# Queries and keys transposed in 32x32 blocks by VectorE and exchanged through device memory; exponentials as a task step of their own

## The chip, the cores and the metric

One core of one Trainium2 chip runs the whole program in one launch. The metric is the device time of that launch in microseconds (us); the kernel before has a median of 3285.07 us over three runs (3284.50 to 3285.92). Engines are named as in the profile: PE (TensorE, matrix multiply), PEld (its weight load), DVE (VectorE), ACT (ScalarE), POOL (GpSimd) and SP (SyncE, which only issues DMAs here).

## The reference, cut to what matters

The input is a sequence of 256 tokens of width 2048, float32 throughout. Two blocks follow one another.

```
def first_block(x, ...):
    h = rms_norm(x) ; proj = h @ w_in           # 2048 -> 17488 columns
    # MLA attention, 16 heads: q, k = 128 "nope" + 64 rotary dims, RMS-normed per head, v = 128
    # FoX attention, 16 heads of 128: q, k RMS-normed, bias F_t - F_s from a cumulative forget gate
    y = concat(causal_attention(mla), causal_attention(fox))
    x = x + (y * sigmoid(gates)) @ w_out
    # PEER: 8 heads of product-key top-16 over 16384 one-neuron experts, dense here:
    x = x + (scattered_gates * gelu(h2 @ u.T)) @ v
def hybrid_layer(x, ...):                       # twice
    aq, ak, av, ag, bq, bk, bv, bg, cu, cglu, cg = split(x @ w_in)
    ya = diff_attention(aq, ak, av)   # 4 heads, two softmaxes of 64 dims each, a = p0 - lam * p1
    yb = dilated_attention(bq, bk, bv)  # 8 heads of 128, three dilated windows merged
    yc = conformer_conv(cu, cglu)     # GLU, causal depthwise conv of 31 taps, LayerNorm, swish, pointwise
    y = concat(ya*silu(ag), yb*silu(bg), yc*silu(cg)) @ w_out
    return layer_norm(ALPHA * x + y)
```

## The kernel before

**Jobs.** All large products run as one list of jobs. A job is one tile of weights of 512 x 512 (1 MB, 128 partitions x 2048), or a smaller one. It is cut into four pieces of 128 x 512. `load` brings the tile into a `raw` buffer (four of them, `AHEAD = 4`) by a DMA on SP's queue; `convert` splits each piece into a high part (`hi`, ACT, L208) and the rest (`lo`, DVE, L209), so that three fast matmuls per piece and token half (L260, L261, L263) give float32 accuracy. Eight `hi` and eight `lo` buffers let the conversion run seven pieces ahead of the matmuls (`PIECES = 7`). A piece is six matmuls of 512 columns. The load of job i+4 is issued when the conversion of job i is done.

**Tasks.** Everything else (norms, transposes, attention heads, the convolution) is written as Python generators, the tasks. `Tasks.step` is called once after each piece; such a step is called a tick here. In each of four lanes it continues the first task in the queue that is due, one step per lane and tick. `yield n` makes the task due n ticks later (`yield` alone: `apart`, by default 4), and no more than four tasks of a lane may be started and unfinished at a time. `flush` runs ticks at once, without matmuls between, until the named tasks are done; it stands where a job's `post` or `need` must have a result. The order of the instructions on each engine is the order in which this plan emits them.

**Queries and keys.** After the product of a query or key block (4 heads, 256 tokens) the raw result lies with tokens on partitions, and attention wants it with head dims on partitions. `to_heads` (L505) does this: `transposed` (L223) issues eight 128x128 transposes on PE (L230) in two PSUM tiles of the pool `side`, and ACT copies each half out with the norm's gain (L510, L512, or L185 with the two half masks for the differential keys `ak`). It is called for the 8 FoX blocks (`fox_norm`), the 8 MLA blocks (`mla_group`, where `rope_T` adds four transposes for the rotary part in the same step), the 12 blocks of the two hybrid layers (`heads_post`), and the 4 blocks of PEER queries.

**Attention heads.** `softmax_block` (L527) adds the bias and takes the row maxima on DVE (L533, L535), then the exponentials with their row sums on ACT (L537), all in one step; the reciprocal of the sums on DVE follows in the same step (L564, L1155, L1194). `weights_transposed` (three PE transposes, L544) and `values` come in later steps.

**The expert blocks already use an exchange.** `expert_in_jobs` transposes the activations in 32x32 blocks on DVE (L952), writes them to device memory by a DMA of POOL's queue (L954), and `weights_load` reads them back block by block by four DMAs (L963), so that tokens and experts have changed places.

Of the kernel before, what the change touches and what calls it, by code (L numbers as in the profile page):

```python
# [17 lines left out]
F32 = mybir.dt.float32  # L18
# [92 lines left out]
def hybrid_block_kernel(ctx: ExitStack, tc: tile.TileContext, a: dict, out: bass.AP):  # L111
# [5 lines left out]
    wp = ctx.enter_context(tc.tile_pool(name="wp", bufs=4))  # L117
    s4p = ctx.enter_context(tc.tile_pool(name="s4p", bufs=16))
# [39 lines left out]
    cst = kept([256], name="cst")  # L158
    A.dma_start(out=cst, in_=a["cst"][:, 0:256])
# [11 lines left out]
    ident, maskf = cst[:, 0:128], cst[:, 128:256]  # L171
# [4 lines left out]
    for c0 in (0, 256):  # L176
        V.tensor_copy(out=causal[:, c0:c0 + 128], in_=maskf)
# [125 lines left out]
    S = {}  # L303
# [166 lines left out]
    def forget_bias(g):  # L470
# [4 lines left out]
        mask = maskf[:, None, :].to_broadcast([P, 4, P])  # L475
# [29 lines left out]
    def to_heads(raw, gain):  # L505

        dst = s4([4, T])
        for pv, c in transposed(lambda c, tb: raw[:, tb, c * P:(c + 1) * P], 4):
            if gain is None:
                A.copy(out=dst[:, c:c + 2, :], in_=pv)  # L510
            else:
                A.activation(out=dst[:, c:c + 2, :], in_=pv, func=AF.Copy, scale=gain)  # L512
        return dst

    def fox_norm(key, raw, gain, post):
        def work():
# [6 lines left out]
            S[key] = to_heads(raw, gain)  # L523
            yield END
        return work()

    def softmax_block(sc, b0, b1, sums):  # L527

        pr = s2([384])
        mx, nmax = small(2), small(2)  # L530
# [8 lines left out]
        return pr  # L539
# [18 lines left out]
    def attention(parts, b0, b1, v, y, h):  # L558
# [3 lines left out]
        sums, rs = small(2), small(2)  # L562
        pr = softmax_block(sc, b0, b1, sums)
        V.reciprocal(out=rs, in_=sums)  # L564
        yield
        pts = weights_transposed(pr)
        yield
        o = values(pts, v, h)
        for tb in range(TB):
            V.tensor_scalar(out=y[:, tb, h * P:(h + 1) * P], in0=o[:, tb * P:(tb + 1) * P], scalar1=rs[:, tb:tb + 1],  # L570
                            scalar2=None, op0=OP.mult)
# [59 lines left out]
    def mla_group(g):  # L631
# [13 lines left out]
        def post_q(ps):  # L645
# [3 lines left out]
            def work():  # L649
# [13 lines left out]
                S["mq", g] = (to_heads(raw, vcol("mq")), rope_T(qr, False))  # L663
# [3 lines left out]
        def post_k(ps):  # L667
# [3 lines left out]
            def work():  # L671
# [13 lines left out]
                S["mk", g] = (to_heads(raw, vcol("mk")), rope_T(kr, True))  # L685
# [20 lines left out]
    def merged_task(key, m, scale):  # L706
# [4 lines left out]
        def work():  # L711
            for pv, c in transposed(lambda c, tb: m[:, tb, c * P:(c + 1) * P], 4):
                split_scaled(h[:, c:c + 2, :], l[:, c:c + 2, :], pv, scale)
# [3 lines left out]
    def gate_jobs(kind, g):  # L717
# [9 lines left out]
        def post(ps):  # L727
# [7 lines left out]
            merged_task(("m" + kind, g), z, 0.5)  # L735
# [91 lines left out]
    def peer_q_jobs():  # L827
# [5 lines left out]
        for b in range(4):  # L833
            def post(ps, b=b):
# [3 lines left out]
                def work():  # L838
                    qT = to_heads(raw, None)
# [271 lines left out]
    def layer(ly):  # L1111
# [3 lines left out]
        def heads_post(name, gain):  # L1115
            def post(ps):
                raw = raw_of(ps)

                def work():
                    if name != "ak":  # L1120
                        L[name] = to_heads(raw, gain)
                    else:
                        L[name] = [s4([4, T]), s4([4, T])]
                        for pv, c in transposed(lambda c, tb: raw[:, tb, c * P:(c + 1) * P], 4):
                            for i in range(2):
                                copy_scaled(L[name][i][:, c:c + 2, :], pv, halves[:, i:i + 1])
# [14 lines left out]
        def diff_post(ps):  # L1141
# [5 lines left out]
            def head(h):  # L1147
                q, k = L["aq"], L["ak"]
                prs, rs = [], []
                for c in range(2):  # L1150
                    sc = side()
                    qk(sc, [(q[:, h], k[c][:, h])])
                    sums, r = small(2), small(2)
                    prs.append(softmax_block(sc, *head_bias(h), sums))
                    V.reciprocal(out=r, in_=sums)  # L1155
                    rs.append(r)
                    yield 3
# [23 lines left out]
        def dil_post(b):  # L1181
            def post(ps):
# [5 lines left out]
                def head(h):  # L1188
# [3 lines left out]
                    sums, r = small(2), small(2)  # L1192
                    pr = softmax_block(sc, *head_bias(4 + 4 * b + h), sums)
                    V.reciprocal(out=r, in_=sums)  # L1194
                    yield 7
                    pts = weights_transposed(pr)
                    yield 7
# [409 lines left out]
```

## Time and profile before

| what | value |
|---|---|
| median of three runs | 3285.07 us (3284.50 to 3285.92) |
| the profiled execution, its own time | 3284.75 us |
| its span, first to last instruction | 3283.0 us |
| PE busy | 3258.2 us (99%) |
| PEld busy | 2706.0 us (82%) |
| DVE busy | 2359.3 us (72%) |
| ACT busy | 1743.4 us (53%) |
| POOL busy | 632.1 us (19%) |
| DMA moved | 676.54 MB, 206 GB/s; POOL's queue 60.45 MB |
| granted PE clock, mean | 0.998 of full speed |

The busy time of PE is a union of pipelined matmuls, whose ends are modelled: what an instruction costs PE is read from the starts of the matmuls around it, not from its duration. The span is 1.75 us shorter than the execution's own time. The first block with its attention takes until about 830 us, PEER until about 2310 us, the two hybrid layers the rest.

### The profile page before, as it was taken

What the parts mean: (1) busy time and instruction counts of PE and PEld (TensorE: products, weight loads), DVE (VectorE), ACT (ScalarE), POOL (GpSimd) and SP (SyncE); (2) the same over time, 40 slices, a digit from 0 to 9 for tenths busy, and PEclk for the clock granted to TensorE, in tenths of its full rate; (3) what the DMA queues carried; (4) which work ended last, traced back from release to release, by engine and by line L of the source; (5) the groups of instructions that cost most, each with busy time, mean ns of one, the idle gap of its engine ahead of it and who ended that gap; (6) DMA issues with size and microseconds to landing.
All of it is one profiled execution on the core that took longest, in us unless ns stands there. A gap on an engine that the chain in (4) does not pass through costs nothing.

```text
span 3283.0 us, 42983 instructions
## 1 busy us (share of the span) xinstructions
PE 3258.2 (99%) x15019; PEld 2706.0 (82%) x15020; DVE 2359.3 (72%) x4739; ACT 1743.4 (53%) x3055; POOL 632.1 (19%) x584
## 2 busy tenths in 40 slices
PE   9999999999999999999999999999999999999998
PEld 7888888888888888888888888888888888788886
DVE  6687676776678887555676666767668777778767
ACT  6655555554655555555554444544555554455553
POOL 0000000000007787875232222220000000000000
PEclk9999999999999999999999999999999999999999
DMA  6554555678457777777788788776564455444554
GB/s 247 173 173 148 182 177 186 212 259 277 175 186 218 215 216 221 218 217 217 262 257 250 243 244 243 229 244 210 204 217 167 154 183 208 168 165 165 177 192 142
DMA packets 159897, 676.54 MB, mean 206 GB/s; under 512 B 52000, under 2 KB 68784, under 8 KB 88128
## 3 DMA queue, kind: packets, MB, share of 16 engines
q1 hardware_dynamic: 102416, 613.06, 55.4%
q0 software_dynamic: 56832, 60.45, 8.7%
q8 instruction: 117, 1.92, 0.2%
q14 instruction: 100, 0.82, 0.1%
q10 hardware_dynamic: 432, 0.29, 0.0%
HBM read 635.58 MB, written 38.15 MB: 205 GB/s over the span
## 4 chain that ended last, share of the span: by engine, by line
PE 98%; DVE 2%; issue 0%; ACT 0%; DMA 0%; SPq 0%; DVEq 0%
PE acc L263 31%; PE acc L260 31%; PE acc L261 31%; PE side L230 2%; PE side L578 2%; PE side L544 1%; DVE lo L209 0%; PE side L554 0%; PE side L555 0%; PE side L553 0%; DVE X L1335 0%; PE side L845 0%; DVE X L1340 0%; DVE lst L1320 0%; DMA X<-in_x_dram 0%
## 5 line engine op out<-in xcount | busy, mean ns | idle before, releaser
L209 DVE TENSOR_TENSOR lo<-raw,hi 128x512 fp32r<-128x512 f32 x2244 | 1503.7, 687 | 713.6 <-ACT hi L208 693.7
L208 ACT CAST hi<-raw 128x512 fp32r<-128x512 f32 x2244 | 1369.0, 622 | 1167.5 <-DVE lo L209 605.1
L260 PE MATMUL acc<-hi,xh 128*128 128x512 f32 x2816 | 1119.4, 398 | 2.0 <-ACT xh L1363 0.9
L263 PE MATMUL acc<-hi,xl 128*128 128x512 f32 x2816 | 1097.9, 390 | 2.8 <-DVE xl L209 2.8
L261 PE MATMUL acc<-lo,xh 128*128 128x512 f32 x2816 | 1097.1, 390 | 0.2 <-DVE lo L209 0.2
L260 PE MATMUL acc<-hi,s 128*128 128x512 f32 x1664 | 654.4, 393 | 0.0
L261 PE MATMUL acc<-lo,s 128*128 128x512 f32 x1664 | 647.5, 389 | 0.0
L263 PE MATMUL acc<-hi,s 128*128 128x512 f32 x1664 | 647.0, 389 | 0.0
L263 PEld LDWEIGHTS acc<-hi,xl 128*128 128x128 f32 x2816 | 528.7, 188 | 116.2 <-DVE xl L209 4.1
L260 PEld LDWEIGHTS acc<-hi,xh 128*128 128x128 f32 x2816 | 529.5, 188 | 108.7 <-ACT xh L1363 1.6
L261 PEld LDWEIGHTS acc<-lo,xh 128*128 128x128 f32 x2816 | 529.8, 188 | 105.4 <-DVE lo L209 0.5
L920 POOL DMA_INDIRECT gd<-pick x256 | 426.6, 1666 | 95.5 <-issue 77.0
L263 PEld LDWEIGHTS acc<-hi,s 128*128 128x128 f32 x1664 | 312.3, 188 | 65.5
L261 PEld LDWEIGHTS acc<-lo,s 128*128 128x128 f32 x1664 | 312.6, 188 | 63.4
L260 PEld LDWEIGHTS acc<-hi,s 128*128 128x128 f32 x1664 | 312.5, 188 | 63.2
L963 POOL DMA_DIRECT2D s<-ad x128 | 76.9, 619 | 404.2 <-DVE lo L209 285.8
L537 ACT ACTIVATE s<-s,sm 128x128 f32<-128x128 f32 (+1 forms) x128 | 57.3, 448 | 121.5 <-DVE sm L535 121.5
L1233 DVE SCALAR_TENSOR_TENSOR s<-s,vec,s 128x256 f32<-128x256 f32 x240 | 115.5, 481 | 4.5
L954 POOL DMA_DIRECT2D ad<-s x32 | 28.4, 889 | 367.0 <-DVE s L952 367.0
L966 POOL DMA_DIRECT2D s<-gd x128 | 90.6, 713 | 23.3 <-DMA s<-gd 13.3
L990 DVE TENSOR_TENSOR X<-X,acc 128x512 f32<-128x512 f32 x128 | 81.8, 680 | 0.0
L295 DVE TENSOR_TENSOR X<-X,acc 128x512 f32<-128x512 f32 x112 | 71.8, 680 | 1.1 <-PE acc L263 1.1
(255 smaller groups left out, 1598.9 us busy)
## 6 DMA issues: line engine op xcount, KB each, us to landing
raw<-in_ut_dram SPq DMA_DIRECT2D x128, 1024.0 KB, 5.1
raw<-in_pv_dram SPq DMA_DIRECT2D x128, 1024.0 KB, 5.7
raw<-in_w_dram SPq DMA_DIRECT2D x120, 1024.0 KB, 4.8
raw<-in_win_dram SPq DMA_DIRECT2D x87, 1024.0 KB, 5.0
raw<-in_wout_dram SPq DMA_DIRECT2D x32, 1024.0 KB, 5.1
raw<-in_wo_dram SPq DMA_DIRECT2D x32, 1024.0 KB, 4.8
gd<-s SPq DMA_DIRECT2D x16, 1024.0 KB, 8.8
raw<-in_wpq_dram SPq DMA_DIRECT2D x16, 1024.0 KB, 4.8
```

The lines of the kernel that those rows point to most:

```text
L208: A.copy(out=hi, in_=src)
L209: V.tensor_tensor(out=lo, in0=src, in1=hi.bitcast(F32), op=OP.subtract)
L230: PE.transpose(pv[:, i, tb * P:(tb + 1) * P], src_of(c + i, tb), ident)
L260: PE.matmul(ps[tb], lhsT=lh[:, kc, t], rhs=wh, start=start, stop=False)
L261: PE.matmul(ps[tb], lhsT=lh[:, kc, t], rhs=wl, start=False, stop=False)
L263: PE.matmul(ps[tb], lhsT=ll[:, kc, t], rhs=wh, start=False, stop=stop)
L295: V.tensor_tensor(out=X[:, tb, c], in0=X[:, tb, c], in1=ps[tb], op=OP.add)
L920: G.indirect_dma_start(out=gd.rearrange("p i (n o) -> (p i n) o", o=1), out_offset=bass.IndirectOffsetOnAxis(ap=pick[:, 1, h, k:k + 1].bit ...
L963: G.dma_start(out=aT[32 * q:32 * q + 32], in_=S["ad", g][:, :, q].rearrange("(i r) t x -> r t i x", i=4))
L966: G.dma_start(out=gg[:, q], in_=gd[:, :, g * 4 * 32:(g + 1) * 4 * 32])
L990: V.tensor_tensor(out=X[:, tb, c], in0=X[:, tb, c], in1=ps[tb], op=OP.add)
L1233: V.scalar_tensor_tensor(out=cv[:, c], in0=pad[:, k:k + T], scalar=tapw(k), in1=cv[:, c], op0=OP.mult, op1=OP.add)
```

## The change

`to_heads` no longer uses PE. A new `exchange` transposes the raw block in 32x32 blocks on DVE (two instructions), writes it to device memory by one DMA of POOL's queue, reads it back by four, and leaves the task for 18 ticks; then ACT copies the result into the head layout, one instruction for each destination. The PEER queries keep the PE transposes, written out where they are used. In `mla_group` the rotary transposes `rope_T` now come before the exchange, in the same step.

`softmax_block` is a generator: the exponentials come one tick after the maxima, and the reciprocals move to the step after the next wait. The yields of the heads are shared out anew (FoX and MLA: 1, 4, 4 instead of 4, 4; differential: 1, 2, 1, 2 instead of 3, 3; dilated: 1, 6, 7 instead of 7, 7). The last part of the convolution gets six one-tick yields.

The weights' `raw` buffers go from four to three (`AHEAD = 3`), and the pool `s4` (4 KB per partition each) from 16 to 18 buffers. The mask for the causal bias is loaded straight into `causal` by two DMAs of ACT's queue instead of by two DVE copies. The factor 0.5 of the gates moves from the split of the merged product into the scaling of the attention output.

```diff
-    wp = ctx.enter_context(tc.tile_pool(name="wp", bufs=4))
-    s4p = ctx.enter_context(tc.tile_pool(name="s4p", bufs=16))
+    wp = ctx.enter_context(tc.tile_pool(name="wp", bufs=3))
+    s4p = ctx.enter_context(tc.tile_pool(name="s4p", bufs=18))
...
-    cst = kept([256], name="cst")
-    A.dma_start(out=cst, in_=a["cst"][:, 0:256])
+    ident = kept([128], name="ident")
+    A.dma_start(out=ident, in_=a["cst"][:, 0:128])
...
-        V.tensor_copy(out=causal[:, c0:c0 + 128], in_=maskf)
+        A.dma_start(out=causal[:, c0:c0 + 128], in_=a["cst"][:, 128:256])
...
-    def to_heads(raw, gain):
-
-        dst = s4([4, T])
-        for pv, c in transposed(lambda c, tb: raw[:, tb, c * P:(c + 1) * P], 4):
-            if gain is None:
-                A.copy(out=dst[:, c:c + 2, :], in_=pv)
-            else:
-                A.activation(out=dst[:, c:c + 2, :], in_=pv, func=AF.Copy, scale=gain)
-        return dst
+    def exchange(src):
+        gt = s4([TB, 4, 4, 32])
+        mem = dram.tile([P, TB, 4, P], F32, name=nm("xm"))
+        for tb in range(TB):
+            V.transpose(out=gt[:, tb].rearrange("p q b c -> p b q c"), in_=src[:, tb])
+        G.dma_start(out=mem, in_=gt.rearrange("p t q b c -> p t q (b c)"))
+        back = gt.rearrange("p t i b c -> p t i (b c)")
+        for q in range(4):
+            G.dma_start(out=back[32 * q:32 * q + 32], in_=mem[:, :, q].rearrange("(i r) t x -> r t i x", i=4))
+        yield 18
+        return back.rearrange("p t i (b c) -> p (t i) b c", b=4)
+
+    def by_32(dst):
+        return dst.rearrange("p b (g c) -> p g b c", c=32)
+
+    def to_heads(raw, *gains):
+        back = yield from exchange(raw)
+        dsts = [s4([4, T]) for _ in gains]
+        for dst, gain in zip(dsts, gains):
+            copy_scaled(by_32(dst), back, gain)
+        return dsts if len(dsts) > 1 else dsts[0]
...
-    def softmax_block(sc, b0, b1, sums):
+    def softmax_block(sc, b0, b1):
...
         V.tensor_scalar(out=nmax, in0=mx, scalar1=-1.0, scalar2=None, op0=OP.mult)
+        yield 1
         for i, (c, bias) in enumerate(parts):
...
-        pr = softmax_block(sc, b0, b1, sums)
-        V.reciprocal(out=rs, in_=sums)
-        yield
-        pts = weights_transposed(pr)
+        pr, sums = yield from softmax_block(sc, b0, b1)
+        yield 4
+        pts = weights_transposed(pr)
+        rs = small(2)
+        V.reciprocal(out=rs, in_=sums)
         yield
...
-                S["mq", g] = (to_heads(raw, vcol("mq")), rope_T(qr, False))
+                qr = rope_T(qr, False)
+                S["mq", g] = ((yield from to_heads(raw, vcol("mq"))), qr)
...
+                    yield 1
                     A.activation(out=th, in_=z, func=AF.Tanh, scale=0.5)
+                    yield 1
                     V.scalar_tensor_tensor(out=th, in0=th, scalar=1.0, in1=z, op0=OP.add, op1=OP.mult)
+                    yield 1
                     A.activation(out=h[:, c:c + 2], in_=th, func=AF.Copy, scale=0.5)
...
-    AHEAD, PIECES = 4, 7
+    AHEAD, PIECES = 3, 7
```

## Rows read from the trace of the kernel before

**Rows 1.** The page, part 1: engine, busy us, share, instructions.
```profile
PE 3258.2 (99%) x15019; PEld 2706.0 (82%) x15020; DVE 2359.3 (72%) x4739; ACT 1743.4 (53%) x3055; POOL 632.1 (19%) x584
```

**Rows 2.** The page, part 4: the chain that ended last, by engine.
```profile
PE 98%; DVE 2%; issue 0%; ACT 0%; DMA 0%; SPq 0%; DVEq 0%
```

**Rows 3.** Timeline of PE around one query block: start us, us, engine, line, operation.
```profile
106.17 0.39 PE L263 MATMUL acc<-hi,xl 128*128 128x512 f32 x1
106.40 1.03 PE L230 MATMUL side<-cst,s 128*128 128x128 f32 x8
107.19 0.48 PE L260 MATMUL acc<-hi,xh 128*128 128x512 f32 x1
107.51 0.40 PE L261 MATMUL acc<-lo,xh 128*128 128x512 f32 x1
...
109.78 0.39 PE L263 MATMUL acc<-hi,xl 128*128 128x512 f32 x1
```

**Rows 4.** Timeline of PE around one MLA block with its rotary transposes.
```profile
193.07 0.40 PE L263 MATMUL acc<-hi,xl 128*128 128x512 f32 x1
193.30 1.48 PE L230 MATMUL side<-cst,s 128*128 128x128 f32 x12
...
194.85 0.39 PE L261 MATMUL acc<-lo,xh 128*128 128x512 f32 x1
```

**Rows 5.** Groups of ACT by shape: operation, count, busy us, mean ns, idle before.
```profile
L208 ACT CAST s<-s 128x1024 fp32r<-128x1024 f32 x32 | 33.6, 1050 | 60.7 <-DVE s L975 55.0 <-DMA s<-gd 5.7
L512 ACT ACTIVATE s<-side,vec 128x512 f32<-128x512 f32 x32 | 20.2, 684 | 18.3 <-PE side L230 18.3
L512 ACT ACTIVATE s<-side 128x512 f32<-128x512 f32 x12 | 6.5, 595 | 7.1 <-PE side L230 7.1
```

**Rows 6.** Groups of PE by shape: the transposes of L230.
```profile
L230 PE MATMUL side<-cst,s 128*128 128x128 f32 x464 | 59.7, 273 | 0.2
```

**Rows 7.** Groups of DVE by shape: the 32x32 block transposes.
```profile
L952 DVE STREAM_TRANSPOSE s<-s 128x512 f32<-128x512 f32 x64 | 45.2, 706 | 6.9 <-ACT s L946 4.7 <-DMA gd<-pick 1.3
```

**Rows 8.** Stretches of 10 us: PE, PEld, DVE, ACT, POOL busy, clock, DMA share, GB/s.
```profile
2520.00:2530.00 10.00, 10.00 (x57) 8.55 (x56) 9.86 (x20) 4.60 (x9) 0.00 (x0) 1.00 0.63 211
2560.00:2570.00 10.00, 10.00 (x58) 8.65 (x57) 9.89 (x23) 3.30 (x6) 0.00 (x0) 1.00 0.59 210
```

**Rows 9.** Waits of all engines: us in total, times, longest us.
```profile
ACT s L537 <- DVE sm L535: 121.5, 64, 4.7
...
DVE sm L564 <- ACT s L537: 34.0, 32, 1.1
...
DVE sm L1155 <- ACT s L537: 16.9, 16, 1.1
```

**Rows 10.** Waits of PE alone.
```profile
PE side L230 <- DMA cst<-in_cst_dram: 1.2, 1, 1.2
...
PE acc L261 <- DVE lo L209: 0.2, 1, 0.2
```

**Rows 11.** Groups of POOL by shape: write and read-back of the expert exchange.
```profile
L963 POOL DMA_DIRECT2D s<-ad x128 | 76.9, 619 | 404.2 <-DVE lo L209 285.8 <-PE acc L263 71.5 <-DMA s<-ad 44.6
L954 POOL DMA_DIRECT2D ad<-s x32 | 28.4, 889 | 367.0 <-DVE s L952 367.0
```

**Rows 12.** Timeline of POOL: a write, and who waits for it.
```profile
1579.06 0.53 POOL L954 DMA_DIRECT2D ad<-s  x1 [21.18 <-DVE s L952]
...
1587.39 0.71 POOL L966 DMA_DIRECT2D s<-gd  x1 [3.32 <-DMA ad<-s]
```

**Rows 13.** Timeline of POOL: read-backs, and who waits for one.
```profile
1723.92 1.79 POOL L963 DMA_DIRECT2D s<-ad  x3 [0.19 <-issue]
...
1732.86 1.19 POOL L963 DMA_DIRECT2D s<-ad  x2 [3.07 <-DMA s<-ad]
```

**Rows 14.** Weight loads L1429, issue to landing: whole span, then 1650 to 1800 us.
```profile
DMA to landing us min/median/max: 3.8/5.0/13.1
...
DMA to landing us min/median/max: 4.7/8.3/12.2
```

More of the change, by code (lines that the diff above doesn't have):

```diff
@@ L474, in forget_bias @@
         yield 8
-        mask = maskf[:, None, :].to_broadcast([P, 4, P])
+        mask = causal[:, None, 0:P].to_broadcast([P, 4, P])
         V.tensor_tensor(out=f0, in0=f[:, :, 0:P], in1=mask, op=OP.add)
@@ L522, in work @@
             yield
-            S[key] = to_heads(raw, gain)
+            S[key] = yield from to_heads(raw, gain)
             yield END
         return work()
-    def softmax_block(sc, b0, b1, sums):
+    def softmax_block(sc, b0, b1):
         pr = s2([384])
+        sums = small(2)
         mx, nmax = small(2), small(2)
@@ L538, in softmax_block @@
                          accum_out=sums[:, i:i + 1])
-        return pr
+        return pr, sums
     def weights_transposed(pr):
@@ L561, in attention @@
         qk(sc, parts)
-        sums, rs = small(2), small(2)
-        pr = softmax_block(sc, b0, b1, sums)
+        pr, sums = yield from softmax_block(sc, b0, b1)
+        yield 4
+        pts = weights_transposed(pr)
+        rs = small(2)
         V.reciprocal(out=rs, in_=sums)
-        yield
-        pts = weights_transposed(pr)
         yield
@@ L684, in work @@
                 yield 4
-                S["mk", g] = (to_heads(raw, vcol("mk")), rope_T(kr, True))
+                kr = rope_T(kr, True)
+                S["mk", g] = ((yield from to_heads(raw, vcol("mk"))), kr)
                 yield END
@@ L704, in mla_group, with merged_task @@
         block_jobs([a["wv"][g]], post_v, get=lambda: S["ckv"])
-    def merged_task(key, m, scale):
+    def merged_task(key, m, scale=None):
         h, l = s4([4, T], F32R), s4([4, T], F32R)
@@ L712, in work @@
             for pv, c in transposed(lambda c, tb: m[:, tb, c * P:(c + 1) * P], 4):
-                split_scaled(h[:, c:c + 2, :], l[:, c:c + 2, :], pv, scale)
+                if scale is None:
+                    split(h[:, c:c + 2, :], l[:, c:c + 2, :], pv)
+                else:
+                    split_scaled(h[:, c:c + 2, :], l[:, c:c + 2, :], pv, scale)
             yield END
@@ L838, in work @@
                 def work():
-                    qT = to_heads(raw, None)
+                    qT = s4([4, T])
+                    for pv, c in transposed(lambda c, tb: raw[:, tb, c * P:(c + 1) * P], 4):
+                        A.copy(out=qT[:, c:c + 2, :], in_=pv)
                     yield
@@ L1113, in layer, with heads_post @@
         L = {}
-        def heads_post(name, gain):
+        def heads_post(name, *gains):
             def post(ps):
@@ L1119, in work @@
                 def work():
[L1120 to L1126, printed above, removed]
+                    L[name] = yield from to_heads(raw, *gains)
                     yield END
@@ L1152, in head @@
                     qk(sc, [(q[:, h], k[c][:, h])])
[L1153 to L1157, printed above, removed]
+                    pr, sums = yield from softmax_block(sc, *head_bias(h))
+                    prs.append(pr)
+                    rs.append(sums)
+                    yield 2
+                for sums in rs:
+                    V.reciprocal(out=sums, in_=sums)
                 V.tensor_scalar(out=rs[1], in0=rs[1], scalar1=S["lam"][:, ly:ly + 1], scalar2=None, op0=OP.mult)
@@ L1191, in head @@
                     qk(sc, [(q[:, h], k[:, h])])
[L1192 to L1195, printed above, removed]
+                    pr, r = yield from softmax_block(sc, *head_bias(4 + 4 * b + h))
+                    yield 6
                     pts = weights_transposed(pr)
+                    V.reciprocal(out=r, in_=r)
                     yield 7
@@ L1270, in pw_post @@
         def pw_post(ps):
-            L["yc"] = raw_of(ps)
+            L["yc"] = raw_of(ps, lambda tb: 0.5)
             L["c_t"] = []
@@ L1305, in layer @@
         outs(0, "oa", first=ALPHA)
-        blk(11, lambda ps: silu_gate(ps, lambda: L["yb", 1], "ob1", 0.5, "b1"))
+        blk(11, lambda ps: silu_gate(ps, lambda: L["yb", 1], "ob1", None, "b1"))
         outs(1, "ob0")
@@ L1450, in hybrid_block_kernel @@
     load(0, 4)
-    for i in range(1, AHEAD):
+    for i in range(1, 4):
         load_x(i)
-        load(i)
+        if i < AHEAD:
+            load(i)
     A.dma_start(out=vec[:, VEC["cb"]:], in_=a["vec"][:, VEC["cb"]:])
```

17 lines of the change are left out of this document (8 added, 9 removed).

## The prediction

> **What bounds the kernel now.** I read the shares of busy time first, then the chain of waits, then PE's own timeline. PE is busy 99% of the span, DVE 72%, ACT 53% [rows 1], and PE makes up 98% of the chain that ended last [rows 2]. A busy PE says little by itself, since the ends of its matmuls are modelled, so the third view is needed: on the timeline matmuls of 512 columns start one every 0.227 us (109.78 - 107.51 = 2.27 us for ten of them), and they go on at that pace right up to a burst of transposes and after it [rows 3]. Nothing stands between them. So what comes off PE's list of work comes off the end, one for one, as long as the other engines still feed it.
>
> The kernel's unit of time is the tick, one piece of weights: six matmuls, 6 x 0.227 = 1.36 us. A job is 5.44 us. The conversion may run seven pieces ahead, 9.5 us: this is the cover that PE has against a late ACT or DVE.
>
> **Taken away: the transposes of queries and keys.** The burst of eight in [rows 3] lies between a matmul that starts at 106.17 and one that starts at 107.51, with one further matmul between. Without the burst these two would be 2 x 0.227 = 0.454 us apart, so it costs 1.34 - 0.45 = 0.886 us (the slower first matmul after it is in this). With rotary transposes in the same step there are twelve: 194.85 - 193.07 - 0.454 = 1.326 us [rows 4]. Four more cost 0.44 us, 0.11 us each, so a burst of four that stays behind costs 0.886 - 0.44 = 0.446 us, and taking eight out of twelve saves 0.88 us. The blocks: 8 of FoX and 8 of MLA (32 evictions of half a block with a per-channel gain), 12 in the layers, of which the 6 with a constant scale show 12 evictions [rows 5]; the 4 blocks of PEER queries keep theirs. FoX and the layers: 20 x 0.886 = 17.7 us. MLA: 8 x 0.88 = 7.0 us. Together 24.7 us off PE.
>
> A check from the group of all these transposes: 59.7 us busy for 464 is 0.129 us each, fixed shares included, and 224 of them make 28.8 us; their mean duration is 273 ns [rows 6], but they overlap, and starts decide. I take the 24.7. The Trainium skill ("TensorE: Matmul & The Clock Gate", Part 4: PE-mode transpose) gives about 275 ns for a transpose inside a kernel. As a duration this agrees with the 273 ns; read as a price it would make the gain 224 x 0.275 = 62 us.
>
> **Added on DVE.** Two block transposes of 128x512 for each of 28 exchanges, 0.706 us each in the expert blocks [rows 7]: 28 x 1.41 = 39.5 us of work. DVE has room on average, not everywhere: in the heads of the layers it is busy 9.86 and 9.89 of 10 us, with PE still at 10.00 [rows 8]. Yet the exponentials' own step gives back more there: a reciprocal in the same step as the exponentials makes DVE wait about 1.06 us each time, 34.0 us over 32 heads, and 16.9 us over 16 softmaxes twice (the second row, L1194, is the same again): 68 us; and ACT waits 121.5 us for the maxima [rows 9]. One tick later the maxima are there, and the sums before they are read. So 39.5 us come and up to 68 us of standing go, mostly in the same stretches. PE waited for a `lo` piece 0.2 us in all [rows 10]; I expect no more after. On PE: 0.
>
> The Trainium skill ("VectorE: DVE Perf Modes", Rules for kernel authors) speaks against the edit: a 128x128 transpose belongs on TensorE when PSUM will do as destination. In engine time the rows agree, 1.41 us on DVE against 0.886 us on PE for a block. By that alone the kernel would lose 28 x 0.5 = 14 us; it holds only where DVE is the bound, which is the rival "DVE becomes the bound" below.
>
> **Added on ACT.** Two evictions of 0.684 or 0.595 us become one copy in the 32-wide layout, as the split of the expert weights does it, 1.050 us [rows 5]: a little less work, and no wait for PE before it. On PE: 0.
>
> **Added on POOL and in the queues.** An exchange is a write of 512 KB and four read-backs of 128 KB, issued in 0.889 and 4 x 0.619 = 2.5 us [rows 11], and POOL does almost nothing else in these stages. How long it takes has no row in these stages, so it is bounded by the busier expert stage. A write issued at 1579.06 has landed when POOL goes on at 1587.39: at most 8.3 us [rows 12]. Reads issued from 1723.92 have freed their place at 1732.86: at most 8.9 us [rows 13]. From below, the fastest weight load landed in 3.8 us [rows 14]. So 1.4 + 8.3 + 2.5 + 8.9 = 21 us at most, 1.4 + 3.8 + 2.5 + 3.8 = 11.5 us at least; I take 15. The task leaves 18 ticks, 24.5 us. What is queued behind: on ACT, behind the copy, the conversion of the next pieces; on POOL, behind the read-backs, the next exchange. MLA's key block starts 4 ticks (5.4 us) after its query block, and POOL is free for it only at 1.4 + 8.3 + 2.5 = 12.2 us, 5.4 us late: 26.5 us at the upper bounds, 2 us over, which the 9.5 us of cover take. Forget biases, queued between, have 8 ticks and lie a few us behind a query's exchange; what DVE might wait there is covered too. On PE: 0, bound 0 to 2 us in each of 4 groups.
>
> **Later results.** An exchange keeps its task started for 18 more ticks. Counting the yields by the planner's rules, with at most four started tasks: the MLA heads of group 0 end 4 ticks before the gate that needs them (36 before the change), those of group 3 16 ticks (50), and all others have over 30. The convolution's last step comes 1 tick ahead of its product (7 before); that product reads its last two channel blocks only two ticks later, so about 4 us remain for one ACT copy and one DVE subtraction. No flush has to run ticks. Cost 0, bound 2 x 1.3 us if the last step of the convolution is a tick late.
>
> **Three weight buffers.** A load is now issued two jobs, 10.9 us, ahead of its conversion instead of 16.3. Loads land in 5.0 us at the median and 13.1 at most; in the worst stretch the median is 8.3 us [rows 14]. The longest would hold ACT for 2.2 us, inside the 9.5 us of cover. Cost 0.
>
> **Start and small things.** The first transposes wait for the constants (1.2 us, [rows 10]); their load is halved, two mask loads are added behind. Within 0.3 us either way; I take +0.2. The moved 0.5 changes no count of instructions on the path.
>
> **The sum.** The profiled execution took 3284.75 us (span 3283.0 and 1.75 around it): 3284.75 - 24.7 + 0.2 = 3260.2. The median of the runs lies 0.3 us above that execution: 3260.5 us.
>
> **Rivals.**
> *The exchange comes late* (the slower side). The place is POOL's queue, in order, where the read-back waits for the write. It decides from 24.5 + 9.5 = 34 us from transposes to landing. If each of its transfers landed like the slowest weight load, 13.1 us, one exchange would take 1.4 + 0.9 + 13.1 + 2.5 + 13.1 = 31 us, still covered; but an MLA key block finds POOL busy until 17.9 us, 11 us after its own transposes, and takes 42 us, 8 us too long. Four groups: 32 us, 3260.5 + 32 = 3293 us. It breaks even at 6 us too long. Against it: the landings in [rows 12, 13] are upper bounds from a stage with more traffic.
> *Three buffers starve the conversion.* If the peaks of 13.1 us, one for each of the 15 repeated read-backs of expert weights, found the cover already spent, PE would stand 15 x 2.2 = 33 us, 3294 us; if a third of it shows, 3272 us. Against it: in that stage the conversion waits for free `hi` buffers, so the cover is full.
> *DVE becomes the bound.* For it speak the full stretches [rows 8]. If the 12 exchanges of the layers come on top there and the freed waits lie elsewhere, 12 x 1.41 = 17 us return: 3277 us, still faster. Against it: the waits freed are those of the same heads.
> *A transpose is worth its duration.* 3285 - 62 = 3223 us. The starts in [rows 3, 4] speak against it.
>
> **How the numbers follow.** Forecast 0.80; exchange late 0.04; starved conversion 0.05 (mostly its small form); DVE the bound, in part or whole, 0.10; duration 0.01. The forecast's own range is 3257 to 3266 (0.65 us of a wait beside one rotary burst, the bounds of start, keys and convolution). I extend it towards the third rival: 3257 to 3269. A run of this kernel tells 0.2%, 6.6 us, from nothing, so faster means below 3278.5. Forecast, DVE, the small form of starvation and the duration are faster: 0.92; the late exchange and the full starvation are the slower side, 0.05; between them 0.03.
>
> **What would show it.** Right: the L230 group falls from 464 to 240 and PE's busy time by about 25 us; bursts of eight vanish from the query and key blocks, bursts of twelve become four, 0.45 us; 56 more block transposes of 0.7 us on DVE; POOL 28 x 3.4 = 95 us busier; L537 no longer waits 121 us for the maxima; POOL's queue moves some 29 MB more; the pitch stays 0.227 us. Wrong: PE waits in its list for `hi` or `lo` pieces, above all in the layers' heads or after MLA blocks; ACT idle before the new copy with a DMA as releaser for more than a few us; ACT waiting for `raw` loads between 1650 and 2310 us. A time over 3272 would mean that the work left PE but something else took its place.

## The result and the profile after

The changed kernel takes 3262.26 us (median of 6 runs, 3261.74 to 3263.20) against 3285.78 us (6 runs, 3284.50 to 3287.28) beside it: a ratio of 0.9928, 95% interval 0.9918 to 0.9939. The forecast was 3260.5 us, its range 3257 to 3269.

The page's busy time by engine, of the changed kernel; it answers to [rows 1]:

```profile
PE 3233.4 (99%) x14796; PEld 2681.7 (82%) x14796; DVE 2388.0 (73%) x4793; ACT 1742.9 (53%) x3025; POOL 715.0 (22%) x724
```

Its chain of work that ended last, by engine; it answers to [rows 2]:

```profile
PE 97%; DVE 2%; DMA 1%; issue 0%; ACT 0%; SPq 0%; DVEq 0%; ACTq 0%
```

PE still is the bound, but it has 24.8 us less to do (3258.2 - 3233.4). The groups of the changed lines (busy us, mean ns of one, then idle time before them and what ended it); the third, L229, answers to [rows 6], and the lines have moved: L230 is now L229, L537 is L557.

```profile
L517 POOL DMA_DIRECT2D s<-xm x112 | 67.7, 632 | 138.7 <-DMA xm<-s 60.7 <-PE acc L262 36.0 <-ACT hi L207 17.8
...
L513 DVE STREAM_TRANSPOSE s<-s 128x512 f32<-128x512 f32 x56 | 36.3, 686 | 0.0
...
L229 PE MATMUL side<-ident,s 128*128 128x128 f32 x240 | 32.0, 273 | 0.8 <-DVE s L702 0.8
...
L557 ACT ACTIVATE s<-s,sm 128x128 f32<-128x128 f32 x64 | 25.6, 401 | 42.6 <-DVE sm L554 42.4
...
L184 ACT ACTIVATE s<-s,vec 128x1024 f32<-128x1024 f32 x16 | 18.4, 1148 | 7.0 <-DMA s<-xm 7.0
...
L514 POOL DMA_DIRECT2D xm<-s x28 | 16.4, 584 | 939.4 <-DVE s L513 939.4
```

The reader sees 224 transposes gone from PE, 56 block transposes of 0.686 us on DVE, and the exponentials waiting 42.4 us for the maxima where they waited 121.5 [rows 9]; the 68 us that DVE stood before the reciprocals are gone altogether. ACT waited 7.0 us in all for exchanges to land. POOL is 82.9 us busier (715.0 - 632.1), not 95: a write is issued in 0.584 us, not 0.889. Where twelve transposes stood, four are left (PE's timeline of the changed kernel: start, duration; it answers to [rows 4]):

```profile
196.90 0.40 PE L262 MATMUL acc<-hi,xl 128*128 128x512 f32 x1
197.14 0.60 PE L229 MATMUL side<-ident,s 128*128 128x128 f32 x4
197.49 0.47 PE L259 MATMUL acc<-hi,xh 128*128 128x512 f32 x1
197.81 0.39 PE L260 MATMUL acc<-lo,xh 128*128 128x512 f32 x1
```

From 196.90 to 197.81 are 0.91 us; less two starts of 0.227 that is 0.456 us (0.446 was forecast).

To see where time went, I took the starts of the 13,440 matmuls of 512 columns that make the products from each trace. They come in the same order in every kernel here, so the n-th of one is set against the n-th of another, and a stage runs from one such matmul to another. In the changed kernel the stages end at 850, 2310, 2792 and 3187 us; behind the last of them no run differs by more than 0.1 us. The stage columns come from the one profiled execution of each run (3283.4 us for e4, 3295.3 for e11, 3260.4 for e8, 3339.6 for e5_wait6), so they need not add up to the difference of the medians. In us more (+) or less (-) than in the changed kernel, stage by stage (the changed kernel's own row has the lengths themselves; the start, ahead of block 1, is told of below); the median has its range and runs, the ratio to the kernel before its 95% interval:

| kernel | median us | ratio | block 1 | experts | layer 0 | layer 1 |
|---|---|---|---|---|---|---|
| before | 3285.78 | 1 | +13.1 | 0.0 | +5.2 | +5.3 |
| changed | 3262.26 | 0.9928 | 792.1 | 1460.1 | 482.3 | 394.5 |
| e1_exchange_only | 3297.27 (3295.7 to 3298.8, 6) | 1.0034 [1.0021, 1.0046] | +12.7 | 0.0 | +11.9 | +11.8 |
| e2_split_only | 3285.92 (3284.8 to 3288.5, 10) | 1.0000 [0.9990, 1.0009] | +12.6 | 0.0 | +5.4 | +5.4 |
| e3_dummy_bursts | 3286.09 (3285.5 to 3287.7, 10) | 1.0001 [0.9992, 1.0011] | +13.5 | 0.0 | +5.3 | +5.3 |
| e7_twice_dve | 3266.17 (3264.9 to 3267.8, 4) | 0.9939 [0.9922, 0.9956] | +2.6 | 0.0 | 0.0 | +1.2 |
| e9_conv_one_step | 3264.83 (3264.1 to 3266.6, 4) | 0.9935 [0.9919, 0.9952] | 0.0 | 0.0 | +1.5 | +1.3 |
| e10_heads_one_step | 3296.68 (3290.1 to 3300.8, 10) | 1.0030 [1.0021, 1.0040] | +15.2 | 0.0 | +9.3 | +10.0 |
| e11_bias_later | 3286.73 (3283.2 to 3295.3, 10) | 1.0004 [0.9995, 1.0014] | +14.6 | 0.0 | +8.9 | +10.5 |
| e5_wait6 | 3336.80 (3330.6 to 3339.6, 4) | 1.0146 [1.0129, 1.0163] | +64.5 | 0.0 | +7.6 | +6.0 |
| e5_wait1 | 3476.73 (3475.8 to 3477.8, 4) | 1.0579 [1.0562, 1.0597] | +152.6 | 0.0 | +29.3 | +31.5 |
| e4_two_raws | 3287.76 (3283.4 to 3290.5, 10) | 1.0006 [0.9996, 1.0015] | +7.5 | +5.4 | +5.8 | +0.9 |
| e8_more_exchanges | 3256.47 (3249.5 to 3260.4, 4) | 0.9904 [0.9888, 0.9921] | +8.8 | -3.6 | -3.6 | -2.4 |
| e12_fewer_exchanges | 3249.65 (3248.9 to 3250.4, 4) | 0.9890 [0.9874, 0.9907] | -1.7 | -3.6 | -3.6 | -3.4 |

### The profile page after: what moved, and what is told of

It is laid out like the page before. It is cut to its first block, busy times and chain, and to the rows that moved or that the text cites. A ratio compares the mean times of both kernels' runs of the same rounds, so it can differ in the third digit from the quotient of the medians.

```text
span 3260.0 us, 42822 instructions
## 1 busy us (share of the span) xinstructions
PE 3233.4 (99%) x14796; PEld 2681.7 (82%) x14796; DVE 2388.0 (73%) x4793; ACT 1742.9 (53%) x3025; POOL 715.0 (22%) x724
## 4 chain that ended last, share of the span: by engine, by line
PE 97%; DVE 2%; DMA 1%; issue 0%; ACT 0%; SPq 0%; DVEq 0%; ACTq 0%
PE acc L262 31%; PE acc L259 31%; PE acc L260 31%; PE side L598 2%; PE side L229 1%; PE side L564 1%; DMA raw<-in_win_dram 0%; PE side L575 0%; PE side L574 0%; PE side L573 0%; DVE lo L208 0%; DVE X L1359 0%; PE side L872 0%; DVE X L1364 0%; DVE lst L1344 0%
## 5 line engine op out<-in xcount | busy, mean ns | idle before, releaser
L514 POOL DMA_DIRECT2D xm<-s x28 | 16.4, 584 | 939.4 <-DVE s L513 939.4
L517 POOL DMA_DIRECT2D s<-xm x112 | 67.7, 632 | 138.7 <-DMA xm<-s 60.7
L1017 DVE TENSOR_TENSOR X<-X,acc 128x512 f32<-128x512 f32 x128 | 81.7, 679 | 0.0
```

Of the source, the lines that this page charges most:

```text
L517: G.dma_start(out=back[32 * q:32 * q + 32], in_=mem[:, :, q].rearrange("(i r) t x -> r t i x", i=4))
L1017: V.tensor_tensor(out=X[:, tb, c], in0=X[:, tb, c], in1=ps[tb], op=OP.add)
```

## The experiments

My theory was the prediction's: the gain is the price of the bursts as their neighbours' starts show it, and the exponentials' own step pays for the new work on DVE. The rivals were that the step gains by itself, that DVE has room without it, and that the exchange comes late.

**e3_dummy_bursts: the bursts come back, with no reader.**

```
+        for pv, c in transposed(lambda c, tb: raw[:, tb, c * P:(c + 1) * P], 4):
+            pass
         back = yield from exchange(raw)
```

> The changed kernel plus, ahead of each of the 28 exchanges, the eight PE transposes that it replaced; nobody reads their result. Theory (a burst costs what the starts of the matmuls around it show, and the gain is that alone): 28 x 0.88 = 24.7 us more than 3262.3, 3286 to 3288 us, about 1 to 2 us above the kernel before. Rival 1 (part of the gain came from elsewhere): under 3281 us. Rival 2 (a transpose is worth its duration): 3262 + 61 = 3323 us.

Measured: 3286.09 us, 23.8 more than the changed kernel, all in the stages where the bursts stand (13.5 + 5.3 + 5.3 = 24.1 us). The group of transposes in this run:

```profile
L229 PE MATMUL side<-ident,s 128*128 128x128 f32 x464 | 59.9, 273 | 0.0
```

Its 59.9 us and 273 ns are nearly those of [rows 6] (59.7 and 273); what 224 of them cost is 24 us, not 61. The price was read rightly from the starts.

**e2_split_only: the exponentials' step without the exchange.**

```
         V.tensor_scalar(out=nmax, in0=mx, scalar1=-1.0, scalar2=None, op0=OP.mult)
+        yield 1
         for i, (c, bias) in enumerate(parts):
```

> The kernel before with the step of the exponentials, the moved reciprocals and the one-tick yields of the convolution alone; PE's transposes, four raw buffers and the start of the kernel before stay. Theory (waits of ACT and DVE off PE's path are worth nothing by themselves): 3284 to 3286.5 us, although ACT's wait for the maxima falls from 121 us to under 60 and DVE's waits before the reciprocals go; all 20 bursts of eight still 0.886 us. Rival (part of the 23.5 us comes from this step): below 3281 us.

Measured: 3285.92 us, no difference. ACT's wait for the maxima fell here too:

```profile
ACT s L539 <- DVE sm L536: 40.0, 33, 2.8
```

Nothing came of it, since in the kernel before PE had waited only 0.5 us in all for `hi` and `lo` pieces.

**e1_exchange_only: the exchange without the step.**

```
         V.tensor_scalar(out=nmax, in0=mx, scalar1=-1.0, scalar2=None, op0=OP.mult)
-        yield 1
+        yield from ()
...
         pr, sums = yield from softmax_block(sc, b0, b1)
-        yield 4
-        pts = weights_transposed(pr)
         rs = small(2)
         V.reciprocal(out=rs, in_=sums)
         yield
+        pts = weights_transposed(pr)
+        yield
```

(the other heads and the convolution likewise, as before the change)

> The changed kernel with the step of the exponentials undone: exponentials and reciprocals in the same step as the maxima, yields of the heads as before the change, no one-tick yields in the last part of the convolution; the exchange, three raw buffers and the start stay. Theory (the step is the cover that pays for the new DVE work): in the layers the conversion was only 0.2 to 0.9 us ahead of PE in the kernel before, 12 exchanges add 12 x 1.37 = 16.5 us of DVE work there, so PE waits for lo pieces in the heads of the layers: 3265 to 3279 us, DVE again waits some 50 to 70 us before the reciprocals and ACT over 100 us for the maxima. Rival (DVE has room anyway, the step of the exponentials is worth nothing): 3261 to 3264 us, PE waits for lo under 2 us.

Measured: 3297.27 us, 35 us more than the changed kernel and 11 more than the kernel before. Alone the exchange loses, alone the step does nothing; together they gain 23.5 us. My theory had the sign and at most half the size (17 us), and it looked only at the layers, while block 1 loses 12.7 us as well. PE hardly waits for `lo`; it waits at its own bursts, most of all at the transposes of the attention weights (L564), for exponentials that come late (us in total, times, longest):

```profile
PE side L564 <- ACT s L557: 10.9, 13, 2.8
...
PE acc L260 <- DVE lo L208: 3.3, 6, 0.8
```

After the start, PE's waits in this trace come to 28.6 us against 6.6 in the changed kernel; the rest of the 35 us is in part a lower clock behind the stops (last section) and in part not traced.

**e10_heads_one_step and e9_conv_one_step: which half of the step matters.** e10 undoes the heads alone, e9 takes out only these three yields, in the convolution's last part (a loop of two, so six in each layer):

```
-                    yield 1
                     A.activation(out=th, in_=z, func=AF.Tanh, scale=0.5)
-                    yield 1
                     V.scalar_tensor_tensor(out=th, in0=th, scalar=1.0, in1=z, op0=OP.add, op1=OP.mult)
-                    yield 1
```

> The changed kernel with only the heads undone: exponentials and reciprocals in the step of the maxima again, yields of the heads as before the change; the one-tick yields of the convolution stay. Theory (each head whose ACT and DVE wait for each other eats cover, and the exchange's DVE work is what the cover no longer holds): block 1 loses the same 13 us as with everything undone, the layers 2 to 8 us each, 3280 to 3292 us. Rival 1 (the convolution's step made all the trouble in the layers): 3275 to 3277 us, no loss after 2310 us. Rival 2 (only both together do harm): under 3268 us.

> The changed kernel with only the one-tick yields in the last part of the convolution taken out again, so that its chain of eight handovers between ACT and DVE is one step, as before the change. In the run with everything undone, about 19 of the 35 us were lost around this step (2624 to 2661 us and 3115 to 3139 us). Theory (the step needs some 7.5 us in which neither engine makes a piece of weights, less than the 9.5 us of cover; it cost so much only because the heads had used the cover up): with the heads' step kept, 3262 to 3268 us. Rival (the convolution's step is too long by itself): 3276 to 3282 us, with one PE wait of over 2 us in each layer.

Measured: the heads carry it. Undoing them costs 34.4 us of the 35.0, 4.7 above what I had allowed, and 9.3 and 10.0 us in the layers where I had allowed 8; the convolution's yields are worth 2.6, inside their range. How block 1 loses is seen in e10. First POOL's timeline (start, duration, then idle time before it and what ended it):

```profile
227.12 2.41 POOL L517 DMA_DIRECT2D s<-xm  x4 [7.40 <-DMA xm<-s]
229.43 0.65 POOL L472 DMA_DIRECT2D s<-fd  x1
```

The load of the forget bias (L472) sits behind an exchange whose read-backs had to wait 7.40 us for their write. DVE's timeline, same run:

```profile
237.00 0.69 DVE L475 TENSOR_TENSOR s<-s,causal 128x512 f32<-128x512 f32 x1 [8.66 <-DMA s<-fd]
...
239.42 1.29 DVE L513 STREAM_TRANSPOSE s<-s 128x512 f32<-128x512 f32 x2
...
244.30 0.17 DVE L584 RECIPROCAL sm<-sm 128x2 f32<-128x2 f32 x1 [1.05 <-ACT s L557]
244.81 0.69 DVE L208 TENSOR_TENSOR lo<-raw,hi 128x512 fp32r<-128x512 f32 x1 [0.34 <-ACT hi L207]
...
247.31 0.17 DVE L584 RECIPROCAL sm<-sm 128x2 f32<-128x2 f32 x1 [1.05 <-ACT s L557]
```

DVE stands 8.66 us for that load, makes an exchange's transposes, and then meets heads whose maxima, exponentials and reciprocal hand over to each other: one `lo` piece takes 247.31 - 244.30 = 3.01 us, more than two of PE's ticks of 1.36 us. ACT, at the same place, waits for the maxima:

```profile
243.28 0.40 ACT L557 ACTIVATE s<-s,sm 128x128 f32<-128x128 f32 x1 [5.74 <-DVE sm L554]
```

With the step in place DVE meets the bias at 248.20 us, without a wait, and the heads come at most every second tick, since a lane runs one step a tick and a head's maxima and exponentials are now two steps. I did not separate the handovers that the step takes away from this spreading; both are the step's.

**e11_bias_later: e10 without the wait for the bias.** `yield 8` becomes `yield 20` between the load and the additions.

> The kernel with the heads undone (3296.7 us), but the two additions of the forget bias come 20 ticks after its load is issued instead of 8, so that DVE no longer meets a load that still sits behind an exchange in POOL's queue (DVE waited 11.2 us in two of them, 8.7 at the longest). Theory (that wait and the ones that follow on ACT start the loss in block 1, which was 15.6 us; the layers' 19 us come from the heads themselves): 3285 to 3291 us, the layers unchanged. Rival (the heads' handovers alone take the cover, the wait on the bias is hidden): 3294 to 3298 us.

Measured: 3286.73 us, 10.0 less than e10, as expected. The profiled execution took 3295.3 us, and its row shows less of the gain. Up to 650 us it has 7 us less loss than e10; then DVE waits for a gate bias (L755), whose load POOL issued at 693.12 us behind two exchanges in a row, and PE waits 6.4 us for DVE:

```profile
DVE s L755 <- DMA s<-in_bgate_dram: 9.9, 1, 9.9
```

So by the medians some 10 of the 15 us of block 1 come from a load in POOL's queue that meets an engine without slack; that the rest of block 1 and the layers (+8.9, +10.5) come from the heads is what is left over, and was not tested by itself.

**e7_twice_dve: the block transposes done twice.**

```
-        for tb in range(TB):
+        for tb in (0, 0, 1, 1):
             V.transpose(out=gt[:, tb].rearrange("p q b c -> p b q c"), in_=src[:, tb])
```

> The changed kernel with both block transposes of every exchange done twice, one after the other: 56 more of 0.686 us, 38.4 us more of DVE work, 16.5 us of it in the layers. Theory (the new step left spare DVE time in the heads of the layers; the lead of the conversion is 3.9 us at the least there): 3262 to 3264 us, lead in the layers a little smaller. Rival (DVE is at its limit there): up to 16.5 us more, 3270 to 3279 us, with PE waiting for lo pieces between 2340 and 3200 us.

Measured: 38.4 us more work on DVE cost 3.9 us, 2 above the theory's range and far below the rival's. Layer 0, where DVE was full before [rows 8], lost nothing. At the same matmuls as the first window of [rows 8], the window reads, first in the changed kernel, then in e7 (length, then busy us of PE, PEld, DVE, ACT and POOL, PE's clock, DMA share, GB/s):

```profile
2501.00:2511.00 10.00, 10.00 (x51) 8.34 (x50) 9.36 (x22) 4.82 (x12) 1.80 (x4) 1.00 0.70 243
...
2504.00:2514.00 10.00, 10.00 (x51) 8.37 (x50) 9.82 (x19) 3.93 (x8) 0.58 (x1) 1.00 0.58 217
```

DVE is nearly full in both, yet PE loses nothing there, while e10, with less work on DVE, loses 9.3 us in this layer. I read this so: what decides is not DVE's busy share but whether it stands waiting between its instructions. Block 1 lost 2.6 us in two MLA key blocks, where PE's rotary transposes wait for a DVE product (L702) behind the doubled transposes; the changed kernel waits 0.8 us at one of them:

```profile
PE side L229 <- DVE s L702: 3.2, 2, 2.3
```

The 1.2 us of layer 1 are PE's clock: behind the stop between the layers, which both kernels have (3.2 us from one matmul to the next), 13 matmuls in e7 start 0.43 us apart (granted clock 0.50 from 2799 to 2805 us), in the changed kernel 7. So PE's waits for the doubled work come to the 2.6 us of block 1.

**e5_wait6 and e5_wait1: less time for the exchange to land.** `yield 18` becomes `yield 6` and `yield 1`.

> The changed kernel with 6 ticks (8.2 us) instead of 18 (24.5 us) between an exchange's transposes and the copy that reads it back. Theory (an exchange takes 12 to 20 us from its transposes to its landing, as the writes land in 4 to 9 us and the reads cannot be issued before; the cover takes 9.5 us): ACT waits 3 to 10 us at most of the 28 copies, 100 to 250 us in all against 7.0, and PE loses little of it, 3262 to 3275 us. Rival 1 (it lands within 8 us, the long wait is not needed): ACT waits under 30 us, 3262 us. Rival 2 (the cover does not take it): PE loses over half of ACT's wait, 3300 us and more.

> The changed kernel with 1 tick (1.36 us) instead of 18 between an exchange's transposes and the copy that reads it back. Theory: ACT waits 10 to 18 us at each of 28 copies, 280 to 450 us in all, of which 9.5 us each is covered: PE stands 1 to 8 us each time, 30 to 220 us, with a clock at half after some of the longer stops: 3290 to 3490 us. Rival (an exchange lands within the cover): under 3275 us.

Measured: with one tick all 28 copies wait for their exchange, so the time from the first block transpose to the copy is what an exchange takes: 9.8 to 14.2 us, at the median 11.35. One of them, from the timelines of DVE, POOL and ACT:

```profile
718.38 1.29 DVE L513 STREAM_TRANSPOSE s<-s 128x512 f32<-128x512 f32 x2
719.96 0.56 POOL L514 DMA_DIRECT2D xm<-s  x1 [21.25 <-DVE s L513]
724.88 2.44 POOL L517 DMA_DIRECT2D s<-xm  x4 [4.36 <-DMA xm<-s]
729.81 1.15 ACT L184 ACTIVATE s<-s,vec 128x1024 f32<-128x1024 f32 x1 [13.48 <-DMA s<-xm]
```

The read-backs are issued 3.3 to 7.5 us after the write, and the copy starts 4.8 to 6.3 us after that. ACT waited 341 us in all and PE lost 214, both as expected for one tick. My theory for six ticks fell, and rival 2 holds by the time (3336.80 us): ACT's total wait was in the theory's range, but PE lost about half of it. The waits of e5_wait6 (total us, times, longest):

```profile
PE side L598 <- ACT s L184: 30.9, 6, 8.2
PE acc L259 <- ACT hi L207: 9.5, 5, 3.7
...
ACT s L184 <- DMA s<-xm: 155.0, 25, 13.2
```

PE did not run out of pieces first. It stood at the scores of the next heads (L598), which need the late copy itself and come a few ticks behind it. The seven pieces of cover don't help there: what counts is the distance in ticks from the late step to PE's next burst that reads it. All six of these waits lie in block 1, where ACT waited 88.8 us for exchanges and PE lost 64.5. In the layers ACT waited 66.2 us, PE never at L598, and PE lost 13.6: there the cover took most of it.

**e4_two_raws: two weight buffers instead of three.** `AHEAD = 2`.

> The changed kernel with two raw weight buffers instead of three: a load is issued one job (5.44 us) ahead of its conversion. Landings took 5.0 us at the median and 8.3 at the median of the worst stretch in the kernel before. Theory (the lead over the landing is what three buffers leave over; with two the mean landing exceeds it where DMA is busiest): ACT waits for raw up to 2.9 us in a job, 256 expert jobs, up to 740 us; over the whole kernel 3300 to 3900 us, and the loss between 830 and 2310 us. Rival (loads land faster than the rows say, so that one job of lead is enough): under 3275 us.

Measured: 3287.76 us, 25.5 more; neither theory. ACT waited for loads in every stage:

```profile
ACT hi L207 <- DMA raw<-in_ut_dram: 178.5, 73, 5.7
ACT hi L207 <- DMA raw<-in_pv_dram: 167.0, 65, 8.2
ACT hi L207 <- DMA raw<-in_win_dram: 97.6, 41, 6.4
```

This is some 620 us with the smaller groups, and PE lost 21.6 us in this trace: ACT is busy 51% of the time here and catches up. How long the loads took to land this profile does not show. Two buffers are too few by 25.5 us; that three are enough is seen in the changed kernel itself, whose experts take as long as with four (0.0 in the table).

**e8_more_exchanges and e12_fewer_exchanges: more bursts replaced.** Where a result is not needed for 18 ticks, the same exchange takes the place of PE's burst:

```
+        def by_exchange():
+            back = yield from exchange(m)
+            h, l = s4([4, T], F32R), s4([4, T], F32R)
+            S[key] = (h, l)
...
-                    qT = s4([4, T])
-                    for pv, c in transposed(lambda c, tb: raw[:, tb, c * P:(c + 1) * P], 4):
-                        A.copy(out=qT[:, c:c + 2, :], in_=pv)
+                    qT = yield from to_heads(raw, 1.0)
```

> The changed kernel with 17 more exchanges in place of bursts of eight PE transposes, where the result is needed 18 ticks later or more: the two latent blocks, four blocks of PEER queries, the merged products of gates m0, f0, f1 and the four of each layer; the constants are loaded as before the change. Theory: 17 x 0.886 = 15.1 us off, and 0.8 us at the start: 3262.3 - 15.9 = 3246.4 us, 3245 to 3249. Rival (DVE has 3.9 us of lead left in the layers; eight exchanges there bring 11 us of DVE work and a larger eviction): part comes back as waits for lo pieces in the layers, 3250 to 3262 us. Second rival (POOL's queue makes some merge late for its product): PE waits of several us in block 1 or the layers, above 3255 us.

Both runs also load the constants as before the change, which is worth 0.8 us at the start. In e8 the head gain of the differential attention is multiplied in ahead of the exchange, where partitions are tokens instead of head dims, so that part of the result is not the reference's; the work is the same in kind. e12 applies the gain behind the exchange. Measured for e8: 3256.47 us, so the second rival holds; PE waited for `lo` pieces only 0.2 us, so the first does not. The gains came, but in the profiled execution one late copy in block 1 held PE for 8.6 us (ACT's timeline, then PE's wait):

```profile
356.53 1.15 ACT L185 ACTIVATE s<-s,vec 128x1024 f32<-128x1024 f32 x1 [9.45 <-DMA s<-xm]
...
PE side L602 <- ACT s L185: 8.6, 1, 8.6
```

POOL's timeline of e8:

```profile
315.29 0.58 POOL L518 DMA_DIRECT2D xm<-s  x1 [14.83 <-DVE s L517]
323.09 2.41 POOL L521 DMA_DIRECT2D s<-xm  x4 [7.22 <-DMA xm<-s]
325.40 0.64 POOL L518 DMA_DIRECT2D xm<-s  x1
334.26 2.41 POOL L521 DMA_DIRECT2D s<-xm  x4 [8.22 <-DMA xm<-s]
336.57 0.65 POOL L518 DMA_DIRECT2D xm<-s  x1
348.06 2.41 POOL L521 DMA_DIRECT2D s<-xm  x4 [10.85 <-PE acc L263]
```

Three exchanges in a row: the second and third write go out the moment POOL is done with the read-backs ahead of them (325.40, 336.57), each exchange holds the queue for 10 to 11 us, and the third lands too late. This is the rival "the exchange comes late", brought about. The four runs spread from 3249.5 to 3260.4 us, and the profile is the one of 3260.4: it does not come out alike each time.

> The changed kernel with 14 more exchanges in place of bursts of eight PE transposes: the four blocks of PEER queries, the merged products of gates m0 and f1, the four of each layer (with the head gain applied behind the exchange); the constants are loaded as before the change. Left on PE against the run with 17: the merged product of f0, whose exchange was the first of three in a row in POOL's queue and cost 10.7 us, and the two latent blocks, which gained nothing. Theory: 14 x 0.886 = 12.4 us and 0.8 at the start off, 3262.3 - 13.2 = 3249.1 us, 3248 to 3252 with a wait of about 1 us in each layer. Rival (the third exchange in a row was not the cause of the 10.7 us): PE waits again for a query or key copy in block 1, 3256 to 3262 us.

Measured: 3249.65 us, as expected (3249.1), 12.6 us below the changed kernel and 36 below the kernel before. In block 1 its trace takes 10.5 us less than e8's (8.8 + 1.7), so with one exchange of the row of three left out (and the two of the latent blocks, early on) the loss is gone. The busy times of e12:

```profile
PE 3221.7 (99%) x14684; PEld 2670.8 (82%) x14684; DVE 2403.1 (74%) x4819; ACT 1742.1 (54%) x3011; POOL 760.4 (23%) x794
```

PE has another 11.7 us less to do, and no new wait of PE came.

## Why the prediction was right, step by step

**The bursts (24.7 us).** Right: e3 puts them back for 23.8 us. In the changed kernel's trace the layers gain 5.2 and 5.3 us (6 x 0.886 = 5.3 forecast), block 1 gains 13.1 of 14.1: there one of PE's rotary bursts waits 0.8 us for DVE (L702), a wait that the sum did not have; the range allowed 0.65 us for one.

**DVE (0).** Right in the result and in naming the step: 56 transposes of 0.686 us are hidden, and without the exponentials' step they are not (e1, e10). That the freed waits do it, and not the spreading of the heads over more ticks, was argued and is not shown. The rival "DVE becomes the bound" was sized at 17 us for the layers; without the step they lose 19.3 us (e10), and block 1, which the rival left out, 15.2. The Trainium skill ("VectorE: DVE Perf Modes", Rules for kernel authors) gives a 128x128 transpose to TensorE when PSUM will do; by these runs that holds for this kernel as long as the heads run in one step (e1 is 11 us slower than before), and no longer once they do not (the changed kernel is 23.5 us faster than before, e12 36).

**ACT (0).** Right; the copy with a channel's gain takes 1.148 us, 0.1 more than assumed.

**The exchange (0, 15 us in 24.5).** The 0 was right, the terms behind it only in part. By itself an exchange took 11.35 us at the median, not 15, and 16 of the 28 took less than the 11.5 that the prediction gave as the least. Where exchanges queue up on POOL, it was close: at its upper bounds it gave an MLA key block behind its query block 26.5 us. In the changed kernel two copies wait, and they start 25.9 and 26.8 us after their first transpose, the second of them such a key block:

```profile
238.51 1.15 ACT L184 ACTIVATE s<-s,vec 128x1024 f32<-128x1024 f32 x1 [4.24 <-DMA s<-xm]
...
702.25 1.15 ACT L184 ACTIVATE s<-s,vec 128x1024 f32<-128x1024 f32 x1 [2.76 <-DMA s<-xm]
```

The cover took these two, as forecast: PE waited for neither. But the cover is not there everywhere. The prediction let 9.5 us of pieces take any late exchange and put the turning point at 34 us; by that rule e5_wait6, with an exchange of 11.35 us against 8.2 us of ticks, loses nothing, and its 28 exchanges cost 74.5 us. With 18 ticks only two copies came late, and by little, so the rule was hardly used: as far as it goes, that is luck, and e8 shows how near the harm is. The prediction's "PE waits in its list for `hi` or `lo`" was the wrong place to look: a late engine shows first at PE's small bursts.

**Later results, three buffers (0).** Right. The forget biases behind exchanges, counted as covered, are so only with the step (e10), and so are the gate biases, which the prediction does not name (e11). With three buffers ACT did wait for weights in the experts, 5.8 us in all, up to 2.8 at a time, where 2.2 had been allowed; the prediction had listed that as a sign of being wrong, but PE lost nothing by it.

**Start (+0.2).** Mis-sized: +0.8 us between the two traces. The 191st of the matmuls starts at 57.20, 57.50, 57.20 and 56.68 us in the profiles with the old start (before, e2, e12, e8) and at 57.42 to 58.51, mean 58.04, in nine with the new one and three raw buffers: 0.9 us between the means, with a scatter as large.

The sum of 24.5 us against 23.0 us in the spans is made up, but for rounding, by these two: 0.6 us at the start and 1.0 us in block 1.

## What to carry to other kernels

Price an operation of the bounding engine by the starts of its neighbours, and put it back as a dummy to check. An edit that gains nothing alone may be what makes another one pay: test the two apart before dropping either. Cover against a late engine is the distance to the first instruction that reads the late result, not only the work prepared ahead. And every load queued in order behind a transfer chain shares that chain's delay.

## What the runs showed of the hardware

After some stops PE's granted clock fell to half. The windows of e1_exchange_only around its longest wait at L564, in layer 0 (window, its length, busy us and instructions of PE, PEld, DVE, ACT and POOL, PE's clock, DMA share, GB/s):

```profile
2655.00:2660.00 5.00, 1.91 (x9) 1.33 (x9) 3.05 (x9) 2.11 (x5) 0.00 (x0) 0.97 0.00 0
2660.00:2662.00 2.00, 1.78 (x5) 1.33 (x6) 0.98 (x3) 2.00 (x7) 0.00 (x0) 0.50 0.00 0
2662.00:2664.00 2.00, 2.00 (x6) 1.57 (x5) 2.00 (x4) 2.00 (x5) 0.00 (x0) 0.50 0.02 4
...
2666.00:2668.00 2.00, 2.00 (x9) 1.64 (x8) 1.97 (x4) 0.62 (x1) 0.00 (x0) 0.86 0.57 238
```

and PE's timeline there:

```profile
2657.01 0.40 PE L262 MATMUL acc<-hi,xl 128*128 128x512 f32 x1
2660.20 1.18 PE L564 MATMUL side<-ident,s 128*128 128x128 f32 x3 [2.80 <-ACT s L557]
...
2662.46 0.63 PE L259 MATMUL acc<-hi,s 128*128 128x512 f32 x1
2662.89 0.63 PE L260 MATMUL acc<-lo,s 128*128 128x512 f32 x1
```

PE had been busy 1.91 of 5 us; then it ran at 0.50 (1.2 of 2.4 GHz), with a matmul every 0.43 us instead of 0.227, for 11 of them: 2.2 us on top of the wait. In the same run PE was busy only 2.20 of the 4 us from 704 to 708 us, and the clock stayed at 1.00 there; why it fell behind the one stop and not behind the other is not shown. In e5_wait6 the matmuls that start 0.40 to 0.46 us apart take 12 us more than in the changed kernel.

Some of the kernels with late engines scatter more: e10 over 10.7 us in ten runs, where the kernel before, run beside it, spread over 4.8 us in 13; e11 over 12.1 us in ten, e8 over 10.9 in four. Others that lose time do not: e1 over 3.1 us in six, e5_wait1 over 2.0 in four. What makes the difference was not looked into.
